# Gate products moved from GpSimd to VectorE, a second PSUM tile for norm sums, and weight parts made before the output product

## The chip, the cores and the metric

The kernel runs on one core of a Trainium2 chip. The metric is the device time of one execution in microseconds; lower is better. A core has TensorE (PE, the matmuls; its weight loads are listed as PEld), VectorE (DVE), ScalarE (ACT), GpSimd (POOL) and SyncE (SP), which here only issues transfers. Each engine works through its own queue in order and waits on semaphores.

## The reference, cut to what matters

One inference step of a two-layer decoder in fp32: a Mamba-2 layer with an MLP, then a sliding-window attention layer with an MLP, for 1024 prompt tokens, 64 sample tokens and 16 meta tokens (1104 columns). The change touches the end of the Mamba mixer, where the scan's output `y` is gated by `z`, normalised in 8 groups of 256 channels, and multiplied by `w_out`:

```
def gated_group_rmsnorm(y, z, w):
    g = (y * jax.nn.silu(z)).astype(jnp.float32)
    g = g.reshape(shp[:-1] + (N_GROUPS, shp[-1] // N_GROUPS))
    g = g * lax.rsqrt(jnp.mean(g * g, axis=-1, keepdims=True) + EPS)
    return (g.reshape(shp) * w.astype(jnp.float32)).astype(y.dtype)
...
    zxbcdt = rmsnorm(h, norm_w) @ w_in
    z = zxbcdt[..., :D_INNER]
...
    out = gated_group_rmsnorm(y, z, gate_w) @ w_out
```

Since silu(z) = z * (1 + tanh(z/2)) / 2, the kernel computes z * (1 + tanh(z/2)) * y and takes the factor of 2 into the norm (`eps4`).

## The kernel before, in words

Activations lie feature-major: 128 features on the partitions, tokens along the columns, the 1104 columns cut into three chunks `CH` of 384, 384 and 336. Every matmul operand is split into a high and a low part (`fp32r`), and `mm3` (lines 199 to 206) makes three matmuls of each product: high by high (L204), high by low (L205), low by high (L206). The parts of a weight are made by a ScalarE cast and a VectorE subtraction: in `wunit` (L170, L171) for plain weights, in `wparts` (L1047, L1048) for the weights of the two large products that are done with seven block products in place of eight (`block_products`, `down_weights`).

A gate group `g` (`gate_group`, L748) has 256 channels, two halves `j`. For each chunk `c` and half it does:

- 24 matmuls of z into one PSUM tile `g` (a bank);
- on ScalarE tanh(z/2) out of PSUM into `g2` (L762);
- on VectorE (g2 + 1) * z, reading z from PSUM (L763); this ends the use of the bank;
- on GpSimd the product with `y` (L770), in place in the y buffer;
- on ScalarE the square (L771).

Then VectorE adds the two squares (L772), `sum_parts` splits the sum in a high part `msh` (ScalarE, L247) and a low part `msl` (VectorE, L248), and two matmuls with a matrix of constants, L259 and L262, sum over the partitions into a PSUM tile `ms`. These two are put off by the list `due`: `tick` counts two half chunks and then calls `gate_norm`, which copies `ms` into a row buffer `gm` on ScalarE (L795). After the third chunk it takes Ln and Exp of the whole row (L798, L799), scales the group (L802), and `side_sums` forms sums and differences of it (L817, L831) and writes them to DRAM (`z_d`). Groups 6 and 7 are written plainly (`g_d`, L809).

Buffers: there are two buffers for y (`gate_of`, by the parity of `g`), each loaded from DRAM by L754 and free again when its group's `z_d` writes have ended; one `gm`; one `ms` bank; and a ring of 7 banks for z (3 of `banks`, 4 of `more_banks`). `split_ahead` (L182) makes weight parts for later layers between the groups, with a multiplication on GpSimd (L168).

Group 0 runs beside the last group of the scan, groups 1 to 7 after it (`gates_out`, L839). After group 7 the output product begins: `block_products` takes 2 blocks of 4 column strips `p`, each with seven products `i` of 18 matmuls, in the PSUM pairs `a`, `d`, `c`, `b` (`ma`, `md`, `mc`, `mb` in the trace). The seven weight sums of a strip come from the generator `down_weights` one at a time: two loads, then parts of a11; of a21 + a22; of a11 - a21; and so on. The other operand comes from `z_d`, in slots cut out of `S`, `R0` and `A`: slots of `S` can be loaded (L1224) only once the last gate has read `S`, and their parts are made by L1229 and L1230.

The order of instructions on each engine is set by a planner that simulates the program in time when it is built (`schedule_with_timeline_sim`). Matmuls L259 are kept in the program's order among TensorE's (`keep_in_program_order`) from group 1 on. So a changed instruction can move others on all queues.

Of the kernel before, what the change touches and what calls it, by code (L numbers as in the profile page):

```python
# [2 lines left out]

# [26 lines left out]
G = 8  # L30
# [111 lines left out]
class Kernel:  # L142
# [605 lines left out]
    def gate_group(self, g, xs, y, gt, tmp):  # L748


        nc, i = self.nc, self.i
        w = [self.wunit(self.in_tile(2 * g * P + j * P), KT, P) for j in range(2)]
        for j in range(2):
            nc.sync.dma_start(out=y[j], in_=self.y_d[g][:, j])  # L754
        for c, (o, n) in enumerate(CH):
            yv = [t[:, o:o + n] for t in y]
            g2 = gt(c)[:, :, :n]
            for j in range(2):
                pt = self.gps()
                self.mm3(pt[:, :n], [(w[j][0][:, k], w[j][1][:, k]) for k in range(KT)],  # L760
                         [(xs[c][0][:, k, :n], xs[c][1][:, k, :n]) for k in range(KT)])
                nc.scalar.activation(out=g2[:, j], in_=pt[:, :n], func=AF.Tanh, scale=0.5)  # L762
                nc.vector.scalar_tensor_tensor(out=g2[:, j], in0=g2[:, j], scalar=1.0, in1=pt[:, :n],  # L763
                                               op0=ALU.add, op1=ALU.mult)
                if j == 0:
                    self.tick()
                    yield

            for j in range(2):
                nc.gpsimd.tensor_tensor(out=yv[j], in0=g2[:, j], in1=yv[j], op=ALU.mult)  # L770
                nc.scalar.activation(out=g2[:, j], in_=yv[j], func=AF.Square)  # L771
            nc.vector.tensor_tensor(out=g2[:, 0], in0=g2[:, 0], in1=g2[:, 1], op=ALU.add)  # L772
            self.tick()
            parts = self.sum_parts(g2[:, 0], n)
            self.due.append([2, partial(self.gate_norm, g, c, y, parts, tmp)])
            if g == 0 and c < 2:

                self.tick(2)
            yield
# [59 lines left out]
    def gates_out(self, xs, big, cr, co, cb, yps, gate):  # L839

        nc = self.nc
        nn = T // 2
        ya = yps[1]
        for c, (o, n) in enumerate(CH):
            nc.sync.dma_start(out=big[:, :, o:o + n], in_=self.i["x"][:, :, o:o + n])
        R0 = self.R0 = self.pool("R0", ctx=self.cR, right=True).tile([P, 2, 4, T], F32R, name="R0")
        slot = [P, 2, KB, nn]
        A5 = self.pool("A5", ctx=co, right=True).tile(slot, F32R, name="A5")
        size = 2 * KB * nn
        cut = lambda t, n: [t[:, k * size:k * size + size].rearrange("p (e q n) -> p e q n", e=2, q=KB)  # L850
                            for k in range(n)]
        S = cut(self.S.rearrange("p e k n -> p (e k n)"), 5)
        B = cut(R0.rearrange("p e k n -> p (e k n)"), 2)
        slots = [[[(t[:, 0], t[:, 1])] for t in ts] for ts in ([A5] + B + S[:4], [S[4], A5, A5] + S[:4])]
        load, parts = self.side_io(self.rz, slots)
        for g in range(1, G):
            for _ in gate if g == 1 else self.gate_of(g, xs, yps):
                pass
            if g < G - 1:
                self.split_ahead()  # L860
            if g == 4:
                for i in range(3):
                    load(0, i)
            if g in (5, 6):
                for i in ((0,), (1, 2))[g - 5]:
                    parts(0, i)
        cr.close()
        for i in range(3, 7):
            load(0, i)
        cb.close()  # L870
        us = self.pool("us", ctx=co).tile([P, 4, nn], F32, name="us")

        def more(b, p, i):
            if (b, p) != (0, 0):
                return
            if 1 <= i <= 4:
                parts(0, i + 2)
            if i == 5:

                self.pstat = (self.pq, self.CHAIN[0][3], 1, 1024)  # L880
                self.tick(9)
                self.pstat = None
            if i == 6:

                t = ya.tile([P, 4, nn], F32R, tag="y", bufs=1, name="A6")
                rest = self.S.rearrange("p e k n -> p (e k n)")[:, 5 * size:].rearrange("p (q n) -> p q n", q=2)
                slots[1][1] = [(rest, t[:, 0:2]), (t[:, 2:3], t[:, 3:4])]
        self.pq = self.pool("pq", space=PSUM, ctx=co)
        rd = [self.gd.get(g) for g in range(G)]
        self.block_products(self.i["w_outs"], big, us, slots, load, parts, [(0, 3, 4, 5, 6)], [(3, 6, 7, 8, 10)],  # L890
                            (lambda: self.block_load(rd, 3, R0), lambda j: self.block_parts(j, R0)), more, (1, 1))

    def out_last(self, hts, done, norm):

# [335 lines left out]
                nc.vector.tensor_tensor(out=lo, in0=lo.bitcast(F32), in1=hi.bitcast(F32), op=ALU.subtract)  # L1230
        return load, parts

    def block_products(self, w, big, us, slots, load, parts, free, make, last, more, early=(0, 0)):


        nc = self.nc
        nn = us.shape[2]
        qw = nn // 2
        nb = len(slots)
        h = [[big[:, 4 * j:4 * j + 4, i * nn:i * nn + nn] for i in range(2)] for j in range(2)]  # L1240

        def step(b, p, i):

            if b == nb - 1:
                if (p, i) == (0, 0):
                    last[0]()
                if p > 0 and i == 2:
                    last[1](p - 1)
                if p == 3 and i == 5:
                    last[1](3)  # L1250
            else:
                for k in range(2):
                    if i == 0 and p == early[k]:
                        load(b + 1, k)
                if p in (1, 2) and i == 2:
                    parts(b + 1, p - 1)
                if p == 3 and i in free[b]:
                    load(b + 1, free[b].index(i) + 2)
                if p == 3 and i in make[b]:
                    parts(b + 1, make[b].index(i) + 2)  # L1260
            if p == 0 and b and i + 7 in make[b - 1]:
                parts(b, make[b - 1].index(i + 7) + 2)

        tt = lambda out, x, y: nc.vector.tensor_tensor(out=out, in0=x, in1=y, op=ALU.add)  # L1264
        for b in range(nb):
            for p in range(4):
                banks = {}
                hv = [[h[j][i][:, p] for i in range(2)] for j in range(2)]
                uv = us[:, p]
                for i, (wh, wl) in enumerate(self.down_weights(w[b], p)):  # L1270
                    e = self.CHAIN[p % 2][i]
                    new = e not in banks
                    if new:
                        banks[e] = self.pq.tile([P, 1024], F32, tag=e, bufs=1, name="m" + e)
                    x = [(hi[:, q], lo[:, q]) for hi, lo in slots[b][i] for q in range(lo.shape[1])]
                    for k in range(2):
                        cs = slice(k * qw, k * qw + qw)
                        self.mm3(banks[e][:, 512 + (k - 1) * qw:512 + k * qw], [(wh[:, q], wl[:, q]) for q in range(KB)],
                                 [(hi[:, cs], lo[:, cs]) for hi, lo in x], new)
                    pv = banks[e][:, 512 - qw:512 + qw]  # L1280
                    to = (uv, hv[1][1], hv[1][1], uv, hv[0][0], hv[1][0], hv[0][1])[i]
                    if i == 0 and b == 0:
                        nc.scalar.copy(out=uv, in_=pv)
                    else:
                        tt(to, pv, to)
                    if b == nb - 1 and i in (3, 4, 5):
                        e, to = ((nc.gpsimd, hv[1][1]), (nc.gpsimd, hv[0][1]), (nc.vector, hv[1][0]))[i - 3]
                        e.tensor_tensor(out=to, in0=to, in1=uv, op=ALU.add)  # L1288
                    step(b, p, i)
                    more(b, p, i)  # L1290
# [492 lines left out]
    def first_layer(self, cb):  # L1783
# [6 lines left out]
        with ExitStack() as ch:  # L1790
# [3 lines left out]
            with ExitStack() as cm:  # L1794
                self.fmp = self.pool("fmp", ctx=cm, right=True)
                self.cw = self.pool("cw", ctx=cm, right=True)
                with ExitStack() as c1:
                    xs = self.mixer(c1)
                self.more_banks(cr, 4)
                ya = self.pool("ya", ctx=co)  # L1800
                yps = self.pool("yb", ctx=cz), ya
                gate = self.gate_of(1, xs, yps)
                for _ in range(4):
                    next(gate)
# [222 lines left out]
```

## Time and profile before

| | us |
|---|---|
| median of 3 runs (2907.71 to 2912.49) | 2910.11 |
| the profiled execution | 2907.35 |
| its span, first to last instruction | 2905.5 |
| TensorE busy in the span | 2812.7 |
| VectorE busy | 2065.7 |
| ScalarE busy | 1418.8 |
| GpSimd busy | 513.2 |

The mean granted TensorE clock of the execution is 0.987. Times in the rows are us from the start of the span unless marked ns; `L763` is line 763 of the kernel; `out<-in` are the program's names for what an instruction writes and reads; `<-X` behind an idle time is what ended it.

### The profile page before, as it was taken

The numbers are of one execution on the slowest core, as the hardware profiler recorded it, in microseconds if no ns is written. First come the engines' busy times: TensorE is split into PE (matmuls) and PEld (weight loads), VectorE is DVE, ScalarE is ACT, GpSimd is POOL, SyncE is SP. The second block draws the span as 40 slices with busy tenths as digits, with TensorE's granted clock in tenths as the row PEclk, the third lists the DMA queues.
The fourth block names the chain that finished last, engine by engine and source line by source line (L and its number), as shares of the span: only waits on it lengthen the run. The fifth ranks groups of instructions, "written<-read, shape, count | busy, mean of one in ns | idle before, by whom it ended". The sixth has DMA issues, their size and how long they took to land.

```text
span 2905.5 us, 51403 instructions
## 1 busy us (share of the span) xinstructions
PE 2812.7 (97%) x19895; PEld 2707.2 (93%) x19895; DVE 2065.7 (71%) x3567; ACT 1418.8 (49%) x2742; POOL 513.2 (18%) x707
## 2 busy tenths in 40 slices
PE   8999999989989999999999999999999999999998
PEld 6999999979889999999999999888989999999998
DVE  6788888865567777665578875676687666567786
ACT  6555555554565265445343335555555454423333
POOL 3255555553310100000000022110110000000011
PEclk9999999999999999999999999999999999999998
DMA  3344444447654224434654433547553444523432
GB/s 138 88 129 127 125 125 127 126 120 253 222 204 168 87 91 154 153 136 140 242 198 170 162 106 93 175 150 251 178 191 124 144 142 150 226 104 131 141 105 70
DMA packets 219468, 433.41 MB, mean 149 GB/s; under 512 B 30728, under 2 KB 128392, under 8 KB 216648
## 3 DMA queue, kind: packets, MB, share of 16 engines
q1 hardware_dynamic: 219224, 430.14, 44.8%
q8 instruction: 156, 2.56, 0.4%
q14 instruction: 88, 0.72, 0.1%
HBM read 302.71 MB, written 128.32 MB: 148 GB/s over the span
## 4 chain that ended last, share of the span: by engine, by line
PE 82%; DVE 8%; DMA 4%; ACT 3%; issue 2%; POOL 1%; SPq 0%; DVEq 0%; POOLq 0%; ACTq 0%
PE g L204 11%; PE g L205 11%; PE g L206 11%; PE mc L204 4%; PE mc L206 4%; PE mc L205 4%; PE ma L204 4%; PE ma L206 4%; PE ma L205 4%; PE md L206 3%; PE md L205 3%; PE md L204 3%; PE mb L204 3%; PE mb L206 3%; PE mb L205 3%
## 5 line engine op out<-in xcount | busy, mean ns | idle before, releaser
L204 PE MATMUL g<-S,w 128*128 128x384 f32 (+2 forms) x1584 | 530.1, 335 | 2.0 <-DMA w<-ws_q 0.8
L205 PE MATMUL g<-S,w 128*128 128x384 f32 (+2 forms) x1584 | 531.9, 336 | 0.0
L206 PE MATMUL g<-S,w 128*128 128x384 f32 (+2 forms) x1584 | 528.6, 334 | 2.2 <-DVE w L171 2.2
L1047 ACT CAST w<-s 128x384 fp32r<-128x384 f32 (+1 forms) x272 | 150.5, 557 | 346.4 <-DVE s L1172 85.9
L206 PEld LDWEIGHTS g<-S,w 128*128 128x128 f32 x1584 | 299.9, 189 | 5.0 <-DVE w L171 2.8
L204 PEld LDWEIGHTS g<-S,w 128*128 128x128 f32 x1584 | 299.1, 189 | 4.6 <-issue 1.2
L205 PEld LDWEIGHTS g<-S,w 128*128 128x128 f32 x1584 | 299.5, 189 | 2.9 <-issue 2.4
L1288 POOL TENSOR_TENSOR hh<-hh,us 128x552 f32<-128x552 f32 (+1 forms) x24 | 36.3, 1534 | 1501.5 <-DVE us L1264 1501.5
L204 PE MATMUL ma<-S,w 128*128 128x276 f32 (+1 forms) x808 | 235.4, 291 | 5.9 <-DVE us L1264 5.9
L206 PE MATMUL ma<-S,w 128*128 128x276 f32 (+1 forms) x808 | 235.2, 291 | 0.0
L205 PE MATMUL ma<-S,w 128*128 128x276 f32 (+1 forms) x808 | 234.8, 291 | 0.0
L1048 DVE TENSOR_TENSOR w<-s,w 128x384 fp32r<-128x384 f32 (+1 forms) x272 | 167.0, 618 | 68.5 <-ACT w L1047 68.5
L1047 ACT CAST w<-raw 128x384 fp32r<-128x384 f32 (+1 forms) x204 | 111.7, 556 | 161.4 <-PE mc L206 46.4
L170 ACT CAST w<-raw 128x1024 fp32r<-128x1024 f32 x96 | 100.5, 1049 | 138.9 <-PE g L205 48.2
L204 PEld LDWEIGHTS ma<-S,w 128*128 128x128 f32 x808 | 153.6, 190 | 7.0 <-issue 5.8
L171 DVE TENSOR_TENSOR w<-raw,w 128x1024 fp32r<-128x1024 f32 x96 | 124.1, 1293 | 48.5 <-ACT w L170 36.4
L205 PE MATMUL g<-R,w 128*128 128x384 f32 (+2 forms) x480 | 158.3, 330 | 0.0
L204 PE MATMUL g<-R,w 128*128 128x384 f32 (+2 forms) x480 | 157.8, 329 | 0.0
L206 PE MATMUL g<-R,w 128*128 128x384 f32 (+2 forms) x480 | 157.7, 329 | 0.0
L205 PEld LDWEIGHTS ma<-S,w 128*128 128x128 f32 x808 | 153.9, 190 | 0.0
L206 PEld LDWEIGHTS ma<-S,w 128*128 128x128 f32 x808 | 153.7, 190 | 0.0
L204 PE MATMUL mc<-S,w 128*128 128x276 f32 (+1 forms) x512 | 148.2, 289 | 0.2 <-DVE hh L1264 0.2
(492 smaller groups left out, 8599.4 us busy)
## 6 DMA issues: line engine op xcount, KB each, us to landing
raw<-in_w_up_dram SPq DMA_DIRECT2D x64, 512.0 KB
raw<-in_w_in_dram SPq DMA_DIRECT2D x48, 512.0 KB
raw<-in_w_downs_dram SPq DMA_DIRECT2D x64, 384.0 KB
w<-ws_o SPq DMA_DIRECT2D x48, 512.0 KB
w<-ws_q SPq DMA_DIRECT2D x40, 512.0 KB
ab<-acs_d SPq DMA_DIRECT2D x64, 256.0 KB
S<-t_d SPq DMA_DIRECT2D x18, 828.0 KB
S<-t_e SPq DMA_DIRECT2D x18, 816.0 KB
```

What stands on the lines that cost most here:

```text
L170: nc.scalar.copy(out=wh, in_=raw)
L171: nc.vector.tensor_tensor(out=wl, in0=raw, in1=wh.bitcast(F32), op=ALU.subtract)
L204: mm(out=out, lhsT=wh, rhs=xh, start=(first and k == 0), stop=False)
L205: mm(out=out, lhsT=wh, rhs=xl, start=False, stop=False)
L206: mm(out=out, lhsT=wl, rhs=xh, start=False, stop=(k == n - 1))
L1047: nc.scalar.copy(out=t[:, 0], in_=src)
L1048: nc.vector.tensor_tensor(out=t[:, 1], in0=src, in1=t[:, 0].bitcast(F32), op=ALU.subtract)
L1288: e.tensor_tensor(out=to, in0=to, in1=uv, op=ALU.add)
```

## The change

Four edits. In `gate_group` VectorE multiplies z out of PSUM by y into the y buffer, and then multiplies that by (g2 + 1); the GpSimd product is gone. `more_banks(cr, 3, 2)` takes 3 further banks for z in place of 4, and 2 banks for `ms` in place of 1. In `gates_out`, in the last group, after the first chunk, the next half chunk and the second chunk, the generator of the first strip's weights is advanced by one each time, which issues its two loads and makes the first three of its seven sets of parts; the sets made and the rest of the generator are handed to `block_products` as `w0` for block 0, strip 0.

```diff
--- before.py
+++ after.py
@@ -1,5 +1,6 @@
 from contextlib import ExitStack
 from functools import partial
+from itertools import chain
 
 import concourse.bass as bass
 import concourse.tile as tile
@@ -760,14 +761,14 @@
                 self.mm3(pt[:, :n], [(w[j][0][:, k], w[j][1][:, k]) for k in range(KT)],
                          [(xs[c][0][:, k, :n], xs[c][1][:, k, :n]) for k in range(KT)])
                 nc.scalar.activation(out=g2[:, j], in_=pt[:, :n], func=AF.Tanh, scale=0.5)
-                nc.vector.scalar_tensor_tensor(out=g2[:, j], in0=g2[:, j], scalar=1.0, in1=pt[:, :n],
+                nc.vector.tensor_tensor(out=yv[j], in0=pt[:, :n], in1=yv[j], op=ALU.mult)
+                nc.vector.scalar_tensor_tensor(out=yv[j], in0=g2[:, j], scalar=1.0, in1=yv[j],
                                                op0=ALU.add, op1=ALU.mult)
                 if j == 0:
                     self.tick()
                     yield
 
             for j in range(2):
-                nc.gpsimd.tensor_tensor(out=yv[j], in0=g2[:, j], in1=yv[j], op=ALU.mult)
                 nc.scalar.activation(out=g2[:, j], in_=yv[j], func=AF.Square)
             nc.vector.tensor_tensor(out=g2[:, 0], in0=g2[:, 0], in1=g2[:, 1], op=ALU.add)
             self.tick()
@@ -853,9 +854,13 @@
         B = cut(R0.rearrange("p e k n -> p (e k n)"), 2)
         slots = [[[(t[:, 0], t[:, 1])] for t in ts] for ts in ([A5] + B + S[:4], [S[4], A5, A5] + S[:4])]
         load, parts = self.side_io(self.rz, slots)
+        ahead = []
         for g in range(1, G):
-            for _ in gate if g == 1 else self.gate_of(g, xs, yps):
-                pass
+            for k, _ in enumerate(gate if g == 1 else self.gate_of(g, xs, yps)):
+                if g == G - 1 and k in (1, 2, 3):
+                    if k == 1:
+                        rest = self.down_weights(self.i["w_outs"][0], 0)
+                    ahead.append(next(rest))
             if g < G - 1:
                 self.split_ahead()
             if g == 4:
@@ -888,7 +893,8 @@
         self.pq = self.pool("pq", space=PSUM, ctx=co)
         rd = [self.gd.get(g) for g in range(G)]
         self.block_products(self.i["w_outs"], big, us, slots, load, parts, [(0, 3, 4, 5, 6)], [(3, 6, 7, 8, 10)],
-                            (lambda: self.block_load(rd, 3, R0), lambda j: self.block_parts(j, R0)), more, (1, 1))
+                            (lambda: self.block_load(rd, 3, R0), lambda j: self.block_parts(j, R0)), more, (1, 1),
+                            chain(ahead, rest))
 
     def out_last(self, hts, done, norm):
 
@@ -1230,7 +1236,7 @@
                 nc.vector.tensor_tensor(out=lo, in0=lo.bitcast(F32), in1=hi.bitcast(F32), op=ALU.subtract)
         return load, parts
 
-    def block_products(self, w, big, us, slots, load, parts, free, make, last, more, early=(0, 0)):
+    def block_products(self, w, big, us, slots, load, parts, free, make, last, more, early=(0, 0), w0=None):
 
 
         nc = self.nc
@@ -1267,7 +1273,7 @@
                 banks = {}
                 hv = [[h[j][i][:, p] for i in range(2)] for j in range(2)]
                 uv = us[:, p]
-                for i, (wh, wl) in enumerate(self.down_weights(w[b], p)):
+                for i, (wh, wl) in enumerate(w0 if w0 is not None and (b, p) == (0, 0) else self.down_weights(w[b], p)):
                     e = self.CHAIN[p % 2][i]
                     new = e not in banks
                     if new:
@@ -1796,7 +1802,7 @@
                 self.cw = self.pool("cw", ctx=cm, right=True)
                 with ExitStack() as c1:
                     xs = self.mixer(c1)
-                self.more_banks(cr, 4)
+                self.more_banks(cr, 3, 2)
                 ya = self.pool("ya", ctx=co)
                 yps = self.pool("yb", ctx=cz), ya
                 gate = self.gate_of(1, xs, yps)
```

## The prediction

> **What bounds the kernel now.** I read the page first: one core, and TensorE busy nearly all the time, so the question is where it is not.
>
> ```profile
> span 2905.5 us, 51403 instructions
> PE 2812.7 (97%) x19895; PEld 2707.2 (93%) x19895; DVE 2065.7 (71%) x3567; ACT 1418.8 (49%) x2742; POOL 513.2 (18%) x707
> ```
>
> About 93 us have no matmul. I then cut the span into stretches: the gates of groups 1 to 7 (665 to 860), the start of the output product (865 to 885), and three stretches that matter for the clock. Columns: us, then busy us (instructions) of PE, PEld, DVE, ACT, POOL, granted clock, DMA share, GB/s.
>
> ```profile
> 665.00:694.00 29.00, 29.00 (x173) 28.95 (x172) 16.12 (x24) 12.33 (x19) 8.79 (x8) 1.00 0.61 207
> 665.00:860.00 195.00, 179.00 (x1021) 175.25 (x1019) 109.65 (x150) 107.11 (x170) 53.49 (x46) 0.97 0.63 218
> 712.88:716.29 3.41, 3.41 (x12) 3.41 (x12) 3.38 (x6) 0.32 (x1) 0.00 (x0) 0.50 0.97 305
> 757.25:764.07 6.82, 6.19 (x19) 6.19 (x20) 3.84 (x7) 3.87 (x7) 0.52 (x1) 0.50 1.03 413
> 859.65:873.30 13.65, 9.64 (x38) 8.97 (x39) 12.77 (x16) 11.02 (x13) 2.02 (x2) 0.50 0.98 368
> 865.00:885.00 20.00, 16.83 (x110) 16.00 (x110) 19.74 (x30) 10.42 (x17) 0.00 (x0) 0.79 0.51 185
> ```
>
> The first row is a full pipe: 29/173 = 0.168 us a matmul, so a group of 144 matmuls and 6 of the norm sums needs 25.1 us. Over the gates TensorE is idle 195 - 179 = 16 us, and in three stretches it runs at half clock while looking busy: 6.19/2 = 3.1 us are lost in the second, 9.64/2 = 4.8 in the third. Who TensorE waited for from 660 to 900 (us, times, longest):
>
> ```profile
> PE ms L259 <- ACT gm L795: 10.3, 6, 3.5
> PE ms L262 <- DVE msl L248: 3.2, 3, 1.5
> PE md L204 <- ACT w L1047: 2.3, 1, 2.3
> PE g L206 <- DVE w L171: 2.2, 2, 1.9
> PE md L206 <- DVE w L1048: 0.9, 1, 0.9
> PE ms L259 <- ACT msh L247: 0.9, 1, 0.9
> ```
>
> The largest wait is for the one PSUM tile `ms`: the next sum (L259) waits until ScalarE has copied the last (L795). The md rows are the output product waiting for its second set of weight parts. In order of time:
>
> ```profile
> 712.24 0.44 PE L206 MATMUL g<-S,w 128*128 128x384 f32 x1 [1.87 <-DVE w L171]
> ...
> 757.88 0.69 PE L259 MATMUL ms<-msh,ones_r 128*128 128x384 f32 x1 [3.51 <-ACT gm L795]
> ...
> 840.27 0.45 PE L262 MATMUL ms<-msl,ones_r 128*128 128x384 f32 x1 [1.50 <-DVE msl L248]
> ...
> 860.49 0.69 PE L259 MATMUL ms<-msh,ones_r 128*128 128x384 f32 x1 [2.89 <-ACT gm L795]
> ...
> 867.91 0.60 PE L204 MATMUL md<-R,w 128*128 128x276 f32 x1 [2.27 <-ACT w L1047]
> ```
>
> Each half-clock stretch begins right behind a stall: 1.87 us, 3.51 us and 2.89 us have one, the 1.50 us has none. But the chain of waits does not run through TensorE here:
>
> ```profile
> 733.67 1.28 ACT L798
> ...
> 745.59 9.92 DMA z_d<-gy
> ...
> 800.81 1.28 ACT L798
> ...
> 816.91 5.75 DMA gy<-y_d
> ...
> 822.90 3.96 POOL gy L770 x4
> ...
> 827.42 0.33 ACT gm L795
> 827.76 1.28 ACT L798
> ...
> 841.21 5.52 DMA gy<-y_d
> ```
>
> It is a loop. A group's normalised gate is written out (z_d), which frees one of two y buffers, which lets y of the group after next load, which lets GpSimd multiply, whose squares stand ahead of the next norm's copy on ScalarE. From the norm's L798 at 733.67 to that at 800.81 two turns took 67 us, 33.6 each, against 25.1 for TensorE; the next, to 827.76, took 27.
>
> **The change, part by part.**
>
> *Second `ms` tile.* The six bank waits are 10.25 us (the 10.3 of the list). How much goes depends on when the other half of the sum was ready: its low part (L248) feeds L262 just behind L259.
>
> ```profile
> 755.07 1.06 DVE L248 TENSOR_TENSOR msl<-n,msh 128x384 fp32r<-128x384 f32 x1
> ...
> 787.39 1.09 DVE L248 TENSOR_TENSOR msl<-n,msh 128x384 fp32r<-128x384 f32 x1
> ...
> 845.28 0.51 DVE L248 TENSOR_TENSOR msl<-n,msh 128x336 fp32r<-128x336 f32 x1 [0.54 <-ACT msh L247]
> ...
> 860.20 0.55 DVE L248 TENSOR_TENSOR msl<-n,msh 128x384 fp32r<-128x384 f32 x1
> ```
>
> In the four short waits (10.25 - 3.51 - 2.89 = 3.85 us together; 787.39 and 845.28 are the low parts of the first and the last) it was done before, so all of that goes. In the 3.51 us wait it ended at 756.13, so 757.88 - 756.13 = 1.75 goes. In the 2.89 us wait it ended at 860.75, after the stall, so some 0.2 goes. Sum 5.8 us; bounds 0 (the order on TensorE is planned anew, and the stall moves to the parts) and 10.25 (the parts come earlier too). I take 5.8.
>
> *Half clock.* The 757 stretch follows a stall that would shrink to 1.76 us, between 1.87 (tripped) and 1.50 (did not): of 3.1 us I take half, 1.5. The 859.65 stretch stays, since its stall stays: 0 of 4.8. The Trainium skill (TensorE: Matmul & The Clock Gate, section "Why this matters for your kernels") asks for no idle gaps over about 3 us; here 1.87 us was enough, so the trace decides. By the page's figure 1.76 us would be safe, and the sum would have 3.1 in place of 1.5.
>
> *z times y from PSUM on VectorE, none on GpSimd.* 48 GpSimd multiplications go, 48 on VectorE come; L763 becomes a multiplication of two SBUF tiles, like L772.
>
> ```profile
> L763 DVE SCALAR_TENSOR_TENSOR n<-n,g x42: 490/546/556, 665.0 to 860.7; 128x384 f32<-128x384 f32 x28, 128x336 f32<-128x336 f32 x14
> L770 POOL TENSOR_TENSOR gy<-n,gy x42: 896/1017/2757, 670.2 to 861.5; 128x384 f32<-128x384 f32 x28, 128x336 f32<-128x336 f32 x14
> L772 DVE TENSOR_TENSOR n<-n x21: 496/550/1201, 683.6 to 864.0; 128x384 f32<-128x384 f32 x14, 128x336 f32<-128x336 f32 x7
> ```
>
> VectorE gains 42 x 0.53 = 22 us on 109.65 of the 195: 56% becomes about 70%. Behind the arrival of y stood one GpSimd step of 1.02 us; now two VectorE steps of 0.55 stand there, because the addition of 1 comes after the product. A wash in the loop: 0. New is a wait at the head of VectorE's queue:
>
> ```profile
> POOL gy L770 <- DMA gy<-y_d: 15.1, 7, 5.4
> ```
>
> GpSimd waited 15.1 us in seven places for y, with nothing urgent behind it. VectorE has behind it the low parts that TensorE waits for and the norms' subtractions whose transfers drive the loop. It costs only where the planner puts the product earlier than y really comes. Already VectorE was late three times (3.2 us). I scale that by its load, 3.2 x 22/110 = 0.6, add 0.4 for these waits, and take -1.0; bounds +4.1 (3.2 + 0.9: no late part any more) and -15.1 (all of the wait lands on a part). The product cannot run beside the tanh that reads the same bank, as these two show (VectorE, then ScalarE, on `tp`: 180.99 + 0.41 = 181.40, next start 181.44):
>
> ```profile
> 180.99 0.41 DVE L641 TENSOR_TENSOR xdt<-tp,dt 80x256 f32<-80x256 f32 x1
> 181.44 0.26 ACT L644 COPY Bt<-tp 80x128 f32<-80x128 f32 x1 [1.48 <-DVE xdt L641]
> ```
>
> So tanh, product and the addition stay in a row, as costed. The Trainium skill (PSUM — Partial Sum Buffer, "PSUM bank collisions raise a hardware error") says that two engines may not read one bank at once; the trace agrees. With GpSimd off, the L772 kind loses its slow cases (1201 against 550 ns); some us of VectorE, which I leave as reserve.
>
> *Six banks for z in place of seven.* No z matmul waits for a bank in the list. A bank is now held until y is there: 5.4 us longer at worst, of a turn of six tiles x 24 x 0.168 = 24 us. 0.
>
> *First weight parts in the last gate.* Moved: two loads of 384 KB, three additions or subtractions, three casts, three low parts. The second load stood on SP's queue behind the loads of S:
>
> ```profile
> 861.43 0.44 SPq L1224 DMA_DIRECT2D S<-z_d  x1
> 861.96 27.23 SPq L1160 DMA_DIRECT2D raw<-in_w_outs_dram  x6
> ```
>
> A step of these parts on VectorE costs 0.55 us:
>
> ```profile
> L1048 DVE TENSOR_TENSOR w<-raw,w 128x384 fp32r<-128x384 f32 x4 | 2.1, 551 | 0.0
> ```
>
> Moved ahead of these loads (and of those that write g_d), the pair of loads lets the second and third set be ready: the md waits go, 2.3 + 0.9 = 3.2 us. It also takes six VectorE steps of 0.55, 3.3 us, out of 865 to 885, where VectorE is busy 19.74 of 20: there the parts of S become late next, and I give back 1.0. In the last gate the same 3.3 us, and three casts on ScalarE, lie where TensorE has its own matmuls; if they delay that gate's low parts, that is within the bound of -15.1. Third set: its tile is one that the last gate's weights hold until its last chunk, so it is made last; 0.
>
> Sum: 5.8 + 1.5 - 1.0 + 3.2 - 1.0 = 8.5 us faster. The profiled execution took 2907.35 us, so 2898.9; the median of the runs is 2.8 above it, so **2901.6**.
>
> **The rivals.**
> 1. *All stalls go.* The parts come early enough: 10.25 + 3.1 + 4.8 + 4.1 + 3.2 = 25.4 us, 2885. For it: GpSimd's 2.76 us cases vanish. Against: the loop's DMAs, 9.92 and 5.75 us in the rows above, stay.
> 2. *The y loop sets the pace.* The plan changes but y of group 7 arrives when it did (841.21 + 5.52 = 846.7), and the sums of that group follow as before; the bank waits turn into waits for low parts. Only the weight parts pay: 3.2 - 1.0 = 2.2 us, 2908. For it: the chain above; against: the last turn took 27 us, little over 25.1, and TensorE's own stalls are in it.
> 3. *VectorE waits for y.* The product stands at the head of VectorE's queue, and all 15.1 us land on low parts or norms, with two more half-clock stretches of 3.41 us (1.7 each): -8.5 + 15.1 + 3.4 = 10 us slower, 2920. It decides once more than some 8.5 of the 15.1 land there. Against: the planner can put ready work ahead.
>
> **How the numbers follow.** Forecast 0.40, with its own range 2893 to 2908; rival 1 0.22, rival 2 0.22, rival 3 0.16. About 0.2% (5.8 us) can be told from no change: below 2904.3 lie three quarters of the forecast, rival 1 and a tenth of rival 2, 0.54; above 2915.9 rival 3 and a little of the forecast and of rival 2, 0.20; the rest 0.26. From rival 1 to short of rival 3's full price: 2884 to 2918.
>
> **What would show it.** Right: no L259 wait for L795; gates' idle near 8 us; the half clock behind group 3 gone, the one near 860 still there; no md wait for L1047. Wrong: waits for msl that grow by as much as the bank waits shrink (rival 2), VectorE idle for gy<-y_d with parts behind it (rival 3), or full clock into the product (rival 1). A new order in stages far away would break the sum altogether.

## The result, and the profile after

| | before | after |
|---|---|---|
| median of the runs, us | 2909.97 (2907.71 to 2912.49) | 2888.89 (2888.53 to 2893.53) |
| profiled execution, us | 2907.35 | 2889.1 |
| its span, us | 2905.5 | 2887.0 |

The ratio is 0.9931, 95% interval 0.9914 to 0.9948: 21 us faster. A later comparison (e9 below), with more runs of the kernel before, gave 0.994 (0.9928 to 0.9953), 17 us. One execution each of e5, e7 and e10 ran at a granted clock of 0.67 to 0.80 and took 3206 to 3763 us; the medians below count them, the ratios do not, and as e10's was the profiled one, no stages of e10 are given.

The page of the kernel after has nearly the same engine shares (POOL 16% for 18%, DVE 72% for 71%); the counts show the 48 products that went from GpSimd to VectorE:

```profile
span 2887.0 us, 51424 instructions
...
PE 2805.9 (97%) x19895; PEld 2700.3 (94%) x19895; DVE 2084.4 (72%) x3615; ACT 1417.7 (49%) x2742; POOL 465.4 (16%) x659
```

The stretches of the kernel after: the gates of groups 1 to 7, a stretch at half clock in them, the first strip of the output product, and a stretch at half clock there. Below them are the gates and the first strip of the kernel before, cut at the product's start (columns as in the prediction):

```profile
665.00:846.50 181.50, 174.97 (x1011) 171.61 (x1011) 126.06 (x194) 107.27 (x171) 12.93 (x6) 0.98 0.66 231
802.14:808.95 6.81, 5.86 (x19) 5.86 (x20) 3.66 (x7) 6.09 (x10) 0.00 (x0) 0.50 0.54 202
846.50:868.50 22.00, 18.90 (x131) 18.13 (x130) 19.27 (x26) 12.87 (x17) 0.00 (x0) 0.92 0.66 262
860.16:863.57 3.41, 3.41 (x16) 3.41 (x17) 3.41 (x5) 1.27 (x1) 0.00 (x0) 0.50 0.38 146
...
665.00:861.30 196.30, 179.81 (x1024) 176.03 (x1022) 110.82 (x152) 108.41 (x171) 54.43 (x47) 0.97 0.63 219
861.30:885.40 24.10, 20.93 (x129) 20.10 (x129) 23.20 (x33) 14.44 (x23) 1.08 (x2) 0.75 0.58 217
```

TensorE's idle time in the gates fell from 196.30 - 179.81 = 16.5 to 181.50 - 174.97 = 6.5 us, although VectorE now works 126 us in 181 instead of 111 in 196. Who TensorE waited for from 660 to 900, after:

```profile
PE ms L260 <- ACT msh L248: 6.0, 5, 2.9
PE md L205 <- ACT w L1053: 2.0, 1, 2.0
PE ma L205 <- ACT S L1235: 0.9, 1, 0.9
PE ms L263 <- DVE msl L249: 0.4, 1, 0.4
PE mb L206 <- DVE S L1236: 0.2, 1, 0.2
```

(Lines are one to six higher than before: L260 and L263 are the two sum matmuls, L248 and L249 the parts, L1053 the cast of weight parts, L1235 and L1236 the parts of S.) No sum waits for the copy out of `ms` any more. The sums now wait for their high part, once for long, and the half-clock stretch of 802.14 begins in that stall; the md wait is a different one from before, for the seventh set of parts in place of the second:

```profile
803.09 0.65 PE L260 MATMUL ms<-msh,ones_r 128*128 128x336 f32 x1 [2.94 <-ACT msh L248]
...
859.60 0.39 PE L205 MATMUL md<-S,w 128*128 128x276 f32 x1 [2.04 <-ACT w L1053]
```

Four stages tell where the time went in each profiled execution. They are cut at the end of the scan's last state matmul (`st`), at the product's first matmul (`ma`), and at its 127th (the end of the first strip). Idle and half clock are of the gates alone; half clock is half of TensorE's busy time in such stretches.

| kernel | to the scan's end | gates | first strip | rest | idle in gates | half clock in gates |
|---|---|---|---|---|---|---|
| before | 666.6 | 194.7 | 24.1 | 2020.0 | 16.5 | 5.2 |
| products only (e1) | 665.3 | 189.0 | 23.8 | 2018.2 | 13.5 | 2.1 |
| `ms` tile only (e2) | 668.4 | 186.2 | 26.8 | 2022.4 | 10.0 | 3.4 |
| weight parts only (e3) | 666.8 | 195.1 | 19.0 | 2017.4 | 17.8 | 3.6 |
| products, `ms` (e4) | 667.5 | 180.9 | 28.3 | 2019.0 | 6.1 | 3.0 |
| products, parts (e5) | 665.7 | 191.3 | 18.3 | 2021.1 | 16.5 | 0.4 |
| `ms`, parts (e6) | 667.6 | 186.4 | 22.2 | 2019.8 | 10.2 | 3.4 |
| after | 664.6 | 181.9 | 21.9 | 2018.5 | 6.5 | 2.9 |
| old order on VectorE (e7) | 670.2 | 186.0 | 19.0 | 2021.7 | 10.7 | 1.7 |
| five sets ahead (e8) | 665.4 | 182.3 | 21.8 | 2017.9 | 7.9 | 1.7 |
| after, again (e9) | 664.3 | 182.4 | 21.7 | 2018.7 | 7.4 | 2.6 |
| after, y loaded twice (e11) | 664.4 | 184.4 | 23.2 | 2017.7 | 10.3 | 1.5 |
| product before tanh (e12) | 663.4 | 189.8 | 21.1 | 2021.5 | 13.5 | 1.7 |

Of the 18.5 us between the two spans, 12.8 are gained in the gates, 2.2 in the first strip, 2.0 before the scan's end and 1.5 in the rest. A profiled execution can lie some us from its kernel's median (e3's by 3 us of its time), so differences of 1 or 2 us in one stage are not read. The spans add up: products, `ms` tile and weight parts by themselves shorten the span by 9.2, 1.7 and 7.2 us, 18.1 together, and the whole change by 18.5.

### The profile page after: what moved, and what is told of

It reads as the page before. It is cut to its first block, busy times and chain, and to the rows that moved or that the text cites. A ratio compares the mean times of both kernels' runs of the same rounds, so it can differ in the third digit from the quotient of the medians.

```text
span 2887.0 us, 51424 instructions
## 1 busy us (share of the span) xinstructions
PE 2805.9 (97%) x19895; PEld 2700.3 (94%) x19895; DVE 2084.4 (72%) x3615; ACT 1417.7 (49%) x2742; POOL 465.4 (16%) x659
## 4 chain that ended last, share of the span: by engine, by line
PE 82%; DVE 8%; DMA 4%; ACT 2%; issue 2%; POOL 0%; SPq 0%; DVEq 0%; ACTq 0%; POOLq 0%
PE g L205 11%; PE g L206 11%; PE g L207 11%; PE mc L205 4%; PE mc L207 4%; PE mc L206 4%; PE ma L205 3%; PE ma L206 3%; PE ma L207 3%; PE md L206 3%; PE md L207 3%; PE md L205 3%; PE mb L205 3%; PE mb L207 3%; PE mb L206 3%
## 5 line engine op out<-in xcount | busy, mean ns | idle before, releaser
L1053 ACT CAST w<-s 128x384 fp32r<-128x384 f32 (+1 forms) x272 | 150.4, 557 | 346.4 <-DVE s L1178 85.3
L1054 DVE TENSOR_TENSOR w<-s,w 128x384 fp32r<-128x384 f32 (+1 forms) x272 | 167.1, 619 | 69.3 <-ACT w L1053 69.2
L1053 ACT CAST w<-raw 128x384 fp32r<-128x384 f32 (+1 forms) x204 | 111.8, 556 | 162.7 <-PE mc L207 47.2
L171 ACT CAST w<-raw 128x1024 fp32r<-128x1024 f32 x96 | 100.6, 1048 | 133.6 <-PE g L206 49.0
L172 DVE TENSOR_TENSOR w<-raw,w 128x1024 fp32r<-128x1024 f32 x96 | 122.6, 1277 | 43.9 <-ACT w L171 29.3
```

The lines of the kernel that those rows point to most:

```text
L171: nc.scalar.copy(out=wh, in_=raw)
L172: nc.vector.tensor_tensor(out=wl, in0=raw, in1=wh.bitcast(F32), op=ALU.subtract)
L1053: nc.scalar.copy(out=t[:, 0], in_=src)
L1054: nc.vector.tensor_tensor(out=t[:, 1], in0=src, in1=t[:, 0].bitcast(F32), op=ALU.subtract)
```

## The experiments

The runs stand in three comparisons (e1 to e4, e5 to e8, e9 to e12), each on a chip of its own with the kernel before beside them. Gains in us are worked out from the ratios.

### The three edits one by one, and two together

The first run makes only the products' edit, the second only

```
-                self.more_banks(cr, 4)
+                self.more_banks(cr, 3, 2)
```

the third only the weight parts (`ahead`, `rest` and `w0` of the diff), the fourth the first two.

> Only the products move to VectorE: one ms tile, seven z banks, weight parts as before. My prediction's sum (theory 1, the bank waits): this edit alone costs 0 to 2 us, so 2909 to 2912, and the waits of L259 for the copy stay near 10 us. Theory 2 (the loop through the y buffers sets the pace of the gates, and the GpSimd step was a slow and late link of it): most of the 21 us come from here, 2893 to 2898, with the loads of y for groups 3 to 7 some 15 us closer together than before (before: 120 us from the third to the seventh).

> Only the second ms tile (and six z banks in place of seven); GpSimd still multiplies. Theory 1: 5.8 us for the bank waits and 1.5 for a half-clock stretch, 2901 to 2904. Theory 2: the bank waits turn into waits for the parts of the sums, 2907 to 2912, and the y loads stay as far apart as before.

> Only the first three sets of weight parts in the last gate. My sum gives 2.2 us: 2907 to 2908. If the half-clock stretch at the product's start belonged to the parts as well, 2900 to 2904. If the parts delay the last gate's norm sums, 2911 or more.

> The whole change without the weight parts. If the parts give the 2.2 us of my sum, 2891. If the start of the product (6 us of it in the comparison of the traces) hangs on the parts, 2894 to 2897. Theory 1 and theory 2 differ by the first two runs: under theory 1 this run is the sum of both and the bank part is the larger; under theory 2 it is close to the run with the products alone.

| kernel | median, us | ratio to before, 95% interval |
|---|---|---|
| e1, products only | 2900.15 | 0.9976 (0.9967 to 0.9985) |
| e2, `ms` tile only | 2905.04 | 0.9993 (0.9984 to 1.0001) |
| e3, weight parts only | 2903.22 | 0.9984 (0.9976 to 0.9993) |
| e4, products and `ms` tile | 2898.12 | 0.9967 (0.9955 to 0.9979) |

Of 2908 us (the median of before in this comparison) that is 7.0, 2.0, 4.7 and 9.6. Only e3 came where one of its expectations put it (2900 to 2904, if the half clock at the product's start belongs to the parts); e1 and e2 lie between theirs, and e4 lies above both of its own. Neither theory stands as it was put. The second tile alone gives no gain that its interval tells from none, so theory 1 fails on the time; the products alone give 7 us where theory 2 asked for 10 to 15, with the y loads of groups 3 to 7 116 us apart in place of 120 (theory 2: some 105). In e2, where GpSimd still multiplies, they are 107 us apart: they follow the pace of the gates. The bank waits of e1 stay at 9.3 us, as theory 1 said, so its 5.7 us in the gates come from elsewhere: 3.1 us of half clock, and the 2.2 us wait for the weight part of L171, which is gone. But the stages show that the second tile does in the gates what the prediction had counted: 8.5 us. TensorE's waits in e2:

```profile
PE md L204 <- ACT w L1047: 6.9, 1, 6.9
PE ms L262 <- DVE msl L248: 5.1, 5, 1.6
PE ms L259 <- ACT msh L247: 4.8, 4, 2.5
PE md L206 <- DVE w L1048: 0.9, 1, 0.9
```

The bank waits (10.3 us) are gone and the waits for the parts of the sums have grown from 3.2 + 0.9 to 9.9 us, so 16.5 us of idle became 10.0. Part of the gain is lost behind the gates, in the first row: the product starts 6.7 us earlier (854.6 instead of 861.3), its second product `md` then waits 6.9 us for weight parts, against 2.3 before, and the first strip is 2.7 us longer. (The rest of what is missing, 1.8 us before the scan's end and 2.4 us behind the strip, is too small to be read.) The same in e4, where the strip is 4.2 us longer; TensorE, then VectorE, then SP's queue:

```profile
857.36 0.60 PE L205 MATMUL md<-R,w 128*128 128x276 f32 x1 [6.53 <-ACT w L1053]
...
853.99 1.88 DVE L1236 TENSOR_TENSOR S<-S 128x1656 fp32r<-128x1656 f32 x1 [2.95 <-ACT S L1235]
855.79 0.50 DVE L249 TENSOR_TENSOR msl<-n,msh 128x336 fp32r<-128x336 f32 x1
856.21 1.02 DVE L1172 TENSOR_TENSOR s<-raw 128x384 f32<-128x384 f32 x2
...
824.40 0.43 SPq L1166 DMA_DIRECT2D raw<-in_w_outs_dram  x1
846.98 0.33 SPq L1166 DMA_DIRECT2D raw<-in_w_outs_dram  x1
847.42 2.44 SPq L1230 DMA_DIRECT2D S<-z_d  x5
```

It is not the transfer. The second half of the strip's weights went out at 824.40 and had landed by 830.0 (the load at 846.98 is the next strip's). But the two sums that need it (L1172) stand in VectorE's order behind the low part of S (L1236), and that waits, through ScalarE's cast, for a transfer that can start only behind the last gate. With the weight parts moved (e9) the first of these sums and its low part (L1054) are made inside the last gate:

```profile
839.27 0.55 DVE L1172 TENSOR_TENSOR s<-raw 128x384 f32<-128x384 f32 x1
...
840.80 0.55 DVE L1054 TENSOR_TENSOR w<-s,w 128x384 fp32r<-128x384 f32 x1
```

and the first strip, 28.3 us in e4, takes 21.7.

### The other two pairs, the old order on VectorE, and five sets ahead

```
e5:  self.more_banks(cr, 4)                        # of the changed kernel
e6:  L763 and L770 of the kernel before            # in the changed kernel
e7:  as e6, but
-                nc.gpsimd.tensor_tensor(out=yv[j], in0=g2[:, j], in1=yv[j], op=ALU.mult)
+                nc.vector.tensor_tensor(out=yv[j], in0=g2[:, j], in1=yv[j], op=ALU.mult)
e8:
-                if g == G - 1 and k in (1, 2, 3):
+                if g == G - 1 and k in (1, 2, 3, 4, 5):
```

> The whole change with one ms tile and seven z banks as before. The single runs gave 7.0 us (vector) and 4.7 us (parts): additive, 2896. If the parts pay more once the product starts earlier (theory 4: an earlier start of the product is eaten by the wait for the second set of weight parts, 6.5 to 6.9 us in the two runs with the second ms tile and without the parts), 2893 to 2895, with no wait of md for L1047 or L1053 at the first strip's second product.

> Second ms tile and weight parts, the products on GpSimd. Additive: 2.0 and 4.7 us, 2901. Theory 4: the second tile lets the product start 6.7 us earlier also without the rest, and only the wait for the parts hid it, so with the parts the sum is 10 to 12 us, 2896 to 2898.

> The whole change, but VectorE first adds 1 and multiplies by z out of PSUM, and then multiplies by y: the old order, only the engine is new. If the gain of the products' part comes from GpSimd being out of the chain, the same as the whole change, 2886 to 2891. If it comes from the order (product with y first), it is near the run with GpSimd, 2896 to 2898. In the old order the bank of z does not wait for y and one step of 0.55 us less stands behind the arrival of y, so by that count alone it could be 1 to 2 us faster than the whole change.

> The whole change with five sets of weight parts in the last gate in place of three. After the change there are still 2.9 us of waits in the first strip, 0.9 for the parts of S and 2.0 for the seventh set of weight parts. If the sets are late because ScalarE and VectorE are full at the product's start, two more made ahead take that wait away: 2 us faster, 2886 to 2887. If the two sets push the last gate's sums back, the product starts later: 2890 or more.

| kernel | median, us | ratio to before, 95% interval |
|---|---|---|
| e5, products and parts | 2897.02 | 0.996 (0.9947 to 0.9973) |
| e6, `ms` tile and parts | 2897.19 | 0.9961 (0.9949 to 0.9973) |
| e7, whole, old order on VectorE | 2899.55 | 0.9972 (0.9961 to 0.9983) |
| e8, whole, five sets ahead | 2891.35 | 0.9945 (0.9933 to 0.9957) |

e6 came where theory 4 put it: without the weight parts the second tile is worth 2.0 us, and on top of them 11.3 - 4.7 = 6.6. But the intervals of these two gains overlap (some 2.5 and 4 us to either side), and the stages do not bear the theory out. The second tile shortens the gates by 8.5 us without the parts and by 8.7 with them (e3 to e6), and it lengthens the first strip by 2.7 us without them and by 3.2 with them. With the wait for the second set gone, the strip that starts earlier waits for what comes late next, the seventh set and the parts of S; e6:

```profile
PE md L205 <- ACT w L1053: 1.4, 1, 1.4
PE ma L206 <- DVE S L1236: 1.4, 1, 1.4
```

e5 is near the plain sum of its two edits (11.6 against 11.7), and the products still leave bank waits there, 13.1 us in seven places.

e7 is the surprise. Old order on VectorE is not faster than the old order on GpSimd (e6), and slower than the whole change by an interval that does not touch that of e9 below. In the gates e6 and e7 take 186.4 and 186.0 us, the whole change 181.9 and 182.4. So the engine alone is worth nothing there, and the new order is worth 4 us. That is not all of e7's loss: its profiled execution is 10.0 us longer than that of the kernel after, 5.6 of it before the scan's end (group 0's gate lies there) and 3.2 behind the first strip, with 2.9 gained in the strip, and no run says why. In e7 TensorE waits:

```profile
PE ms L260 <- ACT msh L248: 4.5, 4, 2.2
PE g L207 <- DVE w L172: 3.9, 3, 2.3
PE ms L263 <- DVE msl L249: 2.0, 5, 0.6
```

The 3.9 us for the low parts of the next group's weights (L172) do not occur in the kernel after. What VectorE waited for, in e7 and then in e9:

```profile
DVE n L764 <- ACT n L763: 27.0, 17, 3.8
DVE gy L771 <- DMA gy<-y_d: 12.0, 7, 4.6
```

```profile
DVE gy L803 <- ACT gm L800: 12.6, 5, 4.5
DVE gy L764 <- ACT n L763: 11.1, 8, 3.1
DVE gy L764 <- DMA gy<-y_d: 9.3, 4, 4.8
DVE gy L764 <- issue: 6.7, 2, 4.6
```

In the old order the first VectorE step waits for the tanh 27 us in all; in the new one 11. That suggested the last experiment below.

e8 gains nothing over the whole change: the wait for the seventh set, 13 us into the first strip, stayed to the hundredth (2.04 us). The run tests little, since the planner had already put the casts of the first six sets early: the sixth starts 1.1 us behind the product's start in both kernels, and the seventh 12.5 us behind it, after casts of parts of S on ScalarE.

### The change again, the loop made longer, and the product ahead of the tanh

```
e10 (of before) and e11 (of after):
-            nc.sync.dma_start(out=y[j], in_=self.y_d[g][:, j])
+            for _ in range(2 if g else 1):
+                nc.sync.dma_start(out=y[j], in_=self.y_d[g][:, j])
e12 (of after): the product z * y issued before the tanh
-                nc.scalar.activation(out=g2[:, j], in_=pt[:, :n], func=AF.Tanh, scale=0.5)
                 nc.vector.tensor_tensor(out=yv[j], in0=pt[:, :n], in1=yv[j], op=ALU.mult)
+                nc.scalar.activation(out=g2[:, j], in_=pt[:, :n], func=AF.Tanh, scale=0.5)
```

> The changed kernel itself, beside the three others of this call, for a yardstick on the same chip. The three edits by themselves gave 7.0 + 2.0 + 4.7 = 13.7 us. If they simply add, 2894 to 2896; if the whole is more than the sum, because the parts uncover what the second ms tile gains, 2887 to 2891.

> The kernel before, with each load of y in groups 1 to 7 issued twice into the same buffer, the second after the first: the loop through the y buffers becomes some 5.7 us a turn longer, and nothing else changes. If that loop sets the pace of the gates (my second rival, and theory 2), five turns cost 20 to 30 us: 2928 to 2938. If TensorE's own work and the order of its norm sums set it, with slack in the loop, under 8 us: below 2916.

> The changed kernel with each load of y in groups 1 to 7 issued twice in the same way. In the changed kernel the gates have 9 us of stalls left in place of 21. If they are the loop's, it is now the only thing that paces the gates, and the price is higher than in the kernel before, 25 us or more: 2914 and up. If the loop has slack, under 8 us: below 2897.

> The changed kernel with the product z times y put ahead of the tanh in the program, so that VectorE has the bank first and ScalarE second. If the gain of the new order (4 us in the gates against the old order on VectorE) comes from VectorE waiting less for ScalarE's tanh (11.6 us in place of 27.0), it grows: 2884 to 2888. If ScalarE then waits for y at the head of its queue, with the squares, casts and copies of the sums behind it, the gates get slower: 2893 or more.

| kernel | median, us | ratio to before, 95% interval |
|---|---|---|
| e9, the whole change | 2890.95 | 0.994 (0.9928 to 0.9953) |
| e10, y loaded twice, before | 2912.09 | 1.0006 (0.9997 to 1.0015) |
| e11, y loaded twice, after | 2891.73 | 0.9941 (0.9927 to 0.9955) |
| e12, product before tanh | 2898.24 | 0.9961 (0.9947 to 0.9974) |

e9: the three edits alone add up to 0.0047 of the time, the whole is 0.0060. The intervals are too wide for the excess to be shown by the times, and the spans have none (18.1 and 18.5 us). That the pieces uncover one another is not shown: the parts shorten the first strip by 5.1 us alone, by 4.6 with the second tile, by 5.5 with the products and by 6.4 with both.

e10 and e11 settle the loop: a second load of y a turn costs nothing that can be measured, in either kernel (e10 at most 4.4 us by its interval, where the loop asked for 20 to 30). In e11 the second load for group 7 goes out 12 us later than e9's only one (831.5 and 819.5), and the gates are 2.0 us longer. VectorE waits three times as long for y, and TensorE's idle time in the gates is 10.3 us against 7.4. VectorE's row, then TensorE's:

```profile
DVE gy L765 <- DMA gy<-y_d: 28.8, 10, 9.3
```

```profile
PE ms L260 <- ACT msh L248: 4.0, 2, 3.3
PE ms L263 <- DVE msl L249: 3.2, 2, 2.1
PE g L205 <- DVE gy L765: 2.5, 2, 1.6
```

The third row is the first wait of a z matmul for a bank in this study (a line lower: L765 is the product there): with y that late, six banks are just too few, for 2.5 us. The planner counts the longer load when it sets the order, so what is shown is slack in the loop as it was planned anew. So the chain of waits, which ran through this loop in the kernel before, showed the path that ended last and not what paces the gates.

e12 does not bear out the idea that the gain of the new order lies in VectorE's shorter wait for the tanh, but it does not refute it either: with that wait turned round, a new one comes in, of ScalarE for VectorE,

```profile
ACT n L764 <- DVE gy L763: 25.8, 8, 10.9
```

and the gates take 189.8 us, as the second half of its expectation said.

## Why the prediction was right, and where it was not

The forecast was faster, 2901.6, in 2884 to 2918; measured 2888.9. The direction and the range held; the forecast's own range (2893 to 2908) did not, and the time is nearer to the first rival's 2885. That the sum came out within the range is partly luck: by the single runs the second tile was taken 5.3 us too high (7.3 for 2.0), the products 8.0 us too low (-1.0 for 7.0) and the weight parts 2.5 us too low (2.2 for 4.7). By its steps:

- *Second `ms` tile and half clock, 5.8 + 1.5 = 7.3 us in the gates.* e2 gained 8.5 us there: 6.5 of idle and 1.8 of half clock. The manner was right, since the bank waits went and part of them came back as waits for parts, but the places were others. Of 10.3 us of bank waits 5.8 came back, so 4.5 were gained; 2.2 more came from the wait for L171, which the sum had not counted. The 2.89 us stall ahead of the product, which was to stay, went, and the half clock moved to 719.67 and 801.59. What the sum lacked is that an earlier start of the product is paid back in part: the first strip grew by 2.7 us, since the second set of weight parts was not there.
- *Products on VectorE, a cost of 1.0.* Wrong in sign: 7.0 us of gain alone, 5.7 of it in the gates. Two steps failed. The wait for y at the head of VectorE's queue was priced at 0.4 us, with a bound of 15.1; e11 made it 28.8 us, for 2.0 us of gates and nothing that the times show. And the new order was counted as a wash by the steps behind y; it is worth 4 us of gates. Why is open: not the engine (e7), VectorE's wait for the tanh is neither shown nor ruled out (e12), and the planner's placing differs in all of these kernels.
- *Weight parts, 3.2 - 1.0 = 2.2.* Too small: 4.7 alone. The first strip of e3 is 5.1 us shorter, 2.4 of it less idle time (3.2 to 0.8), as the sum had it, and 2.8 less half clock (4.4 to 1.6), which the sum put at 0. Its reason, that the stretch stays because its stall stays, was half right: in e3 the stall (3.67 us) and the stretch are there, but the stretch lasts 3.41 us in place of 13.65. In the kernel before, TensorE was idle for 25, 24, 62 and 6% of the stretch's four quarters, and all of the idle time in the second and third is the md waits; in e3 it was not idle in the first, and full clock came back behind it. The prediction's reason for the md waits was wrong too: the load in the row of 861.96 is the next strip's. The second load of the first strip had gone out at 832.49, and the sums made from it stood behind the parts of S on VectorE, as in e4.
- *Six banks, 0.* Right: no z matmul waits for a bank in the kernel after, and 2.5 us do when y comes another load later.
- *Rival 2 (the y loop sets the pace)* rested on the chain of waits. e10 and e11 refute it. *Rival 3 (VectorE waits for y)* falls with e11. *Rival 1* had the time nearly right, but not all stalls went: 6.5 us of idle and 2.9 of half clock stay in the gates.

Of what was to show it: no L259 wait for the copy, right; idle of the gates near 8 us, 6.5; the half clock behind group 3 gone, right (another came in the 2.94 us stall at 803); no md wait for the second set, right. The half clock near 860, which was to stay, did not: the product starts at full clock,

```profile
846.50:849.91 3.41, 3.41 (x29) 3.41 (x28) 2.73 (x6) 2.02 (x5) 0.00 (x0) 1.00 1.00 397
```

which was named as a sign for rival 1. The stretch at 860.16 in the kernel after is another one, 14 us into the strip, with the 2.04 us wait for the seventh set.

## What to carry to other kernels

A stage that ends earlier is worth only what the next one can use: look at what is late next (here 2.7 of 8.5 us of gates were lost in the first strip, 4.2 of 13.8 with the products too), and expect another late piece behind the one that is moved. Look up which load a wait hangs on before blaming the queue: here the data had landed long before, and the order on VectorE was late. Test a loop that the chain of waits shows by making it longer: if a second transfer in it costs nothing, it has slack, however often the chain runs through it. When a planner sets the order, an edit's price is not its instructions: the same steps of a gate in another order moved the gates by 4 to 8 us.

## What the runs showed of the hardware

But for the last one of each execution, half-clock stretches in these runs were 3.41 us long or whole multiples (6.8, 10.2 and 13.65 us), and they start on a fixed grid: from 712.88 to 757.25 and from there to 859.65 in the kernel before are 13 and 30 times 3.413 us. Two of these three began before their stall had ended (757.88 and 860.49), so they do not begin behind the stall, as the prediction read it. And stalls of the same length did or did not bring one: in e2 one of 1.57 us did and one of 1.59 us did not, and in e7 one of 2.31 us did, while one of 2.25 us, which lies across two windows of the grid, did not. The window of the first in e7, then the two of the second, with the granted clock as the third number from the end; at 802.89 the clock fell to half:

```profile
799.48:802.89 3.41, 1.42 (x8) 1.42 (x9) 3.41 (x5) 0.88 (x2) 0.00 (x0) 1.00 0.85 262
850.67:854.08 3.41, 2.16 (x15) 1.88 (x13) 2.79 (x5) 1.20 (x3) 0.00 (x0) 1.00 0.67 268
854.08:857.49 3.41, 1.97 (x12) 1.72 (x13) 2.79 (x7) 2.22 (x6) 0.00 (x0) 1.00 1.01 332
```

TensorE was idle for 58% of the first window, and for 37 and 42% of the others. So it is the idle share of a window that counts, more than the length of a stall: in the profiled executions here but e10's, from 600 to 900 us, the window ahead of each stretch was idle for 41 to 100%, and no window idle for over 55% was without one behind it. Half clock went on behind windows idle for 15% or more and ended behind those idle for 16% or less. These bounds are no full rule, since far from the gates less was enough (35% at 1890 us of the kernel before).

The prediction read 1.87 us as a length that trips and 1.50 as one that does not; by these a length alone decides nothing near 2 us. The Trainium skill (TensorE: Matmul & The Clock Gate, section "What's actually happening") describes a free-running window of 3413 ns; the lengths and the starts here agree with it.
